# Rope for the first retention head inside the dense stage of a hybrid block kernel, with a place of its own for the returning values

## The chip, the cores and the metric

The kernel runs on one core of one Trainium2 chip. The metric is the device time of one execution in microseconds (us). The time is the median of several executions; a further execution is taken by the hardware profiler, and all rows that are quoted come from such a profiled execution.

A core has five engines that work side by side, each through its own queue of instructions in order: TensorE (PE in the rows, its weight loads PEld), VectorE (DVE), ScalarE (ACT), GpSimd (POOL) and SyncE (SP). They wait for each other by semaphores. SP, ACT and POOL also issue DMA transfers between the main memory and the core's memory (128 partitions). TensorE writes its results into banks of PSUM.

## The reference

One block of a transformer on 512 tokens and 16 leading meta tokens (528 in all, 1024 wide, fp32):

```python
h = concat(meta, x)
h = h + 0.5 * swiglu(rmsnorm(h, ffn1_norm), ffn1_w_gate, ffn1_w_up, ffn1_w_down)
h = h + hybrid_mixer(rmsnorm(h, mix_norm), pos, k_top, w_in, w_ret_out, w_att_out, w_mix_out)
h = h + 0.5 * swiglu(rmsnorm(h, ffn2_norm), ffn2_w_gate, ffn2_w_up, ffn2_w_down)
y = rmsnorm(h, final_norm)[:, 16:]
```

The mixer projects the tokens with one matrix, `w_in`, into: retention queries and keys (`rq`, `rk`, 4 heads of 256), values (`rv`, 4 heads of 512) and gate (`rg`); attention queries, keys and values (`aq`, `ak`, `av`, 8 heads of 128); index queries and key (`iq`, 8 heads of 64; `ik`, one head) with weights `iw`; and two gates `g_ret`, `g_att` of width 1024. Then

```python
yr = retention(rope(rq), rope(rk) / 16, rv)      # scores with a decay by distance, causal, then rmsnorm
yr = (silu(rg) * yr) @ w_ret_out
ya = attention(rope(aq), rope(ak), av, top 128 keys of each query by the index scores, and the meta tokens) @ w_att_out
merged = sigmoid(g_ret) * yr + sigmoid(g_att) * ya
```

Rope multiplies the two halves of each query or key by cosines and sines: `x1 * cos - x2 * sin`, `x2 * cos + x1 * sin`.

## The kernel before

**Arithmetic.** Each fp32 operand is split into a high and a low part. `split` makes the high part by a copy on ACT and the low part by a subtraction on DVE (L117, L118 in the profile; L278, L279 in the pipelined steps). `mm3` (L145) does three matmuls for each product (L153). The activations of the mixer lie split as `xh`, `xl`; weights are loaded on SP into `raw` (L133, two buffers of 1 MB) and split into `whi`, `wlo` (three buffers).

**Order.** The order on TensorE is that of the program everywhere (a manual schedule for PE). In the dense stage ACT and DVE follow the program too; later a scheduler orders ACT, DVE, POOL and SP. `steps_through` (L283) pipelines the dense steps: each step loads its weights four steps ahead (`pre`), has the high parts made two steps ahead (`upper`) and the low parts beside a step (`lower`).

**The dense stage** (in the mixer up to about 572 us). After the first FFN come nine early steps: index queries and keys, the retention queries and keys of head 0. `normed_out` (L868) multiplies these by the norm and writes them to main memory (`fq`, `fs`, `fk`). Then three units of `Values` compute the values of four retention heads and eight attention heads by Strassen's seven products, 14 steps each, and write them to `vst` and `vd` through POOL's queue. After each of the first two units stands a `gate_step` for the retention gate; after the third stand two `rg_step`s (the first two blocks of head 0's `rg`, left in PSUM as `first_rg`) and a `gate_step` for the first block of the attention gate (GA).

**Retention** (pool `rt`, about 572 to 935 us), head by head. For head 0 the queries and keys are loaded back from `fs` and `fk` with the rope tables, and pass `rope_pair` (L1366): four products on DVE (L1371), two sums on POOL (L1374) and two splits. For the others they come from projections `psrq` and `psrk`, which end in the same function. `load_values` (L1320) loads the head's values from `vst` into one of the two `raw` buffers (L1323) and splits them into `vo`. `decayed` (L1413) computes the scores `psst` (L1422) and multiplies them by the decay (L1426) on DVE. Then, for four blocks, `gated` projects `psrg` and `weigh` (L1445) multiplies scores and values (`pspv`, L1442). `ret_out` (L1381) of one head is done during the next head: it projects with `w_ret_out` (`psro`), multiplies by the norm on DVE (L1400) and adds on POOL into `accr` (L1401).

Between these pieces, `step()` takes one piece of background work: in head 0 the index scores (`index_steps`, L1271, matmuls `pssc` L1285, for which `index_ropes`, L1242, ropes the index queries and keys loaded back from `fq` and `fs`), from head 1 on the selection of the top 128 (`select_steps`, L1295, MAX8 and MATCH_REPLACE8 on DVE).

**Attention** (about 935 to 1160 us). Values come from `load_values` again. For each head `scores` (L1599) computes four blocks `psS` (L1612) in the order 3, 2, 1, 0, the block 3 in a two-bank tile and the others in one-bank tiles, and softmaxes them; the next head's `proj_q` and `proj_k` follow, then `transpose_p`, a `wide_gate` (one block of a gate, 24 matmuls, in a two-bank tile) and `weigh_v`.

The output projection, the second FFN and the last norm follow; the change does not touch them.

## Time and profile before

| what | value |
|---|---|
| time, median of 3 runs | 1604.28 us (1603.66 to 1606.98) |
| the profiled execution's own time | 1602.45 us |
| its span, first instruction to last | 1600.7 us |
| mean granted clock of TensorE | 0.979 of full speed |
| PE busy | 1533.6 us (96%) |
| DVE busy | 1088.7 us (68%) |
| ACT busy | 726.6 us (45%) |
| POOL busy | 169.9 us (11%) |
| read and written in main memory | 155.14 MB and 15.75 MB |

How to read the rows further on. The page shows the span in 40 equal slices of 40 us, each with a digit for the busy share in tenths (9 is 90% or more) or the granted clock. A row of the table of stretches has: begin and end, length, then busy time of PE, PEld, DVE, ACT and POOL with the number of instructions in brackets, the granted clock of TensorE, the share of the DMA engines and GB/s. A row of the waits has: the waiting engine and operation, what it waited for, us in total, times, the longest. A row of the chain of waits has: start, length, what the end of the kernel was waiting for at that time. A row of the timeline has: start, length, engine, line, operation, output and input, and in square brackets the idle time of the engine just before it with what ended it. A row of one line's instructions has the shortest, median and longest duration in ns.

### The profile page before, as it was taken

Reading aid. Unit: us, or ns where it says so; the run is one execution under the profiler, and the core shown is the slowest. Engines: PE = TensorE matmul, PEld = TensorE weight load, DVE = VectorE, ACT = ScalarE, POOL = GpSimd, SP = SyncE. Lnnn points to the kernel's source line nnn. Section 1 sums busy time; section 2 is a strip of 40 time slices with the busy share of each in tenths; the row PEclk is TensorE's granted clock in tenths of the full one; section 3 lists DMA queues with packets and bytes.
Section 4 is the critical chain, followed back from the end, with each engine's and each line's share of the span. In section 5 each row is a group of like instructions: output and inputs, shape, how many; then the busy total and the mean of one; then the engine's idle time right before and its main releaser. Section 6 shows DMA issues by size and latency. Waiting matters only on the chain.

```text
span 1600.7 us, 24057 instructions
## 1 busy us (share of the span) xinstructions
PE 1533.6 (96%) x9779; PEld 1380.9 (86%) x9779; DVE 1088.7 (68%) x1652; ACT 726.6 (45%) x1145; POOL 169.9 (11%) x180
## 2 busy tenths in 40 slices
PE   9999999999999948999898989999999999999998
PEld 8999999999888836878687878888888889899996
DVE  4987685876867647795858356655455688577685
ACT  6564362543444424333233336666435445354353
POOL 0000000012101120203223051120001100000000
PEclk9999999999999978999899999999999999999999
DMA  4233223347155251141413143222434223323232
GB/s 160 80 106 106 93 98 101 106 130 259 67 192 184 80 171 49 53 136 38 154 38 110 60 139 90 72 69 80 139 126 137 79 80 105 132 80 132 79 106 92
DMA packets 154302, 172.42 MB, mean 108 GB/s; under 512 B 5008, under 2 KB 130984, under 8 KB 153424
## 3 DMA queue, kind: packets, MB, share of 16 engines
q1 hardware_dynamic: 143824, 147.49, 28.5%
q10 hardware_dynamic: 6880, 12.84, 2.4%
q0 software_dynamic: 3488, 10.58, 1.6%
q8 instruction: 76, 1.25, 0.3%
q14 instruction: 34, 0.28, 0.1%
HBM read 155.14 MB, written 15.75 MB: 107 GB/s over the span
## 4 chain that ended last, share of the span: by engine, by line
PE 85%; DVE 5%; ACT 3%; issue 2%; DMA 2%; POOL 2%; ACTq 0%; POOLq 0%; DVEq 0%
PE psqX L153 13%; PE psd L153 8%; PE psd L1806 7%; PE psqY L153 6%; PE psrg L153 5%; PE psvX L1071 4%; PE psqZ L153 3%; PE psrk L153 3%; PE psu L153 3%; PE psrq L153 3%; PE psmo L153 3%; PE psat L153 3%; PE psgate L153 3%; PE psak L153 3%; PE psaq L153 2%
## 5 line engine op out<-in xcount | busy, mean ns | idle before, releaser
L118 DVE TENSOR_TENSOR wlo<-raw,whi 128x1024 fp32r<-128x1024 f32 (+1 forms) x122 | 143.7, 1178 | 138.8 <-ACT whi L117 137.8
L117 ACT ACTIVATE whi<-raw 128x1024 fp32r<-128x1024 f32 (+1 forms) x122 | 114.4, 939 | 257.5 <-DMA raw<-in_w_in_dram 40.9
L278 ACT ACTIVATE whi<-raw 128x1024 fp32r<-128x1024 f32 (+2 forms) x138 | 121.4, 881 | 110.2 <-PE psd L153 37.5
L279 DVE TENSOR_TENSOR wlo<-raw,whi 128x1024 fp32r<-128x1024 f32 (+2 forms) x138 | 141.0, 1026 | 33.9 <-ACT whi L278 33.9
L153 PE MATMUL psqX<-th,whi 128*128 128x264 f32 (+1 forms) x432 | 122.3, 283 | 0.0
L153 PE MATMUL psqX<-tl,whi 128*128 128x264 f32 (+1 forms) x432 | 122.3, 283 | 0.0
L153 PE MATMUL psqX<-th,wlo 128*128 128x264 f32 (+1 forms) x432 | 122.2, 283 | 0.0
L278 ACT ACTIVATE whi<-wsum 128x1024 fp32r<-128x1024 f32 x72 | 76.3, 1060 | 70.6 <-PE psd L1806 22.0
L279 DVE TENSOR_TENSOR wlo<-wsum,whi 128x1024 fp32r<-128x1024 f32 x72 | 87.7, 1219 | 12.5 <-ACT whi L278 12.5
L153 PEld LDWEIGHTS psqX<-th,whi 128*128 128x128 f32 x432 | 82.1, 190 | 0.3 <-DVE g L492 0.3
L153 PEld LDWEIGHTS psqX<-tl,whi 128*128 128x128 f32 x432 | 82.0, 190 | 0.0
L153 PEld LDWEIGHTS psqX<-th,wlo 128*128 128x128 f32 x432 | 82.0, 190 | 0.0
L153 PE MATMUL psro<-vo,whi 128*128 128x512 f32 x256 | 79.0, 390 | 0.0
L153 PE MATMUL psd<-hl,whi 128*128 128x264 f32 x352 | 71.3, 284 | 0.0
L153 PE MATMUL psd<-hh,wlo 128*128 128x264 f32 x352 | 70.7, 283 | 0.0
L153 PE MATMUL psd<-hh,whi 128*128 128x264 f32 x352 | 70.7, 282 | 0.0
L1806 PE MATMUL psd<-whi,hh 128*128 128x512 f32 x176 | 68.5, 389 | 0.0
L1806 PE MATMUL psd<-wlo,hh 128*128 128x512 f32 x176 | 68.5, 389 | 0.0
L1806 PE MATMUL psd<-whi,hl 128*128 128x512 f32 x176 | 68.5, 389 | 0.0
L252 POOL TENSOR_TENSOR ssum<-ssum,sq 128x528 f32<-128x528 f32 (+1 forms) x14 | 18.4, 1317 | 443.3 <-ACT sq L251 443.3
L153 PEld LDWEIGHTS psro<-vo,whi 128*128 128x128 f32 x256 | 48.0, 188 | 10.0
L153 PE MATMUL psrg<-xh,wlo 128*128 128x512 f32 x128 | 52.6, 411 | 2.5 <-DVE wlo L118 2.5
(434 smaller groups left out, 4654.1 us busy)
## 6 DMA issues: line engine op xcount, KB each, us to landing
raw<-in_ffn_w_up_dram SPq DMA_DIRECT2D x22, 1024.0 KB, 5.0
raw<-in_ffn_w_gate_dram SPq DMA_DIRECT2D x21, 1024.0 KB, 5.0
raw<-in_w_in_dram SPq DMA_DIRECT2D x19, 1024.0 KB, 4.9
raw<-in_w_in_dram SPq DMA_DIRECT2D x31, 512.0 KB, 3.5
raw<-in_ffn_w_down_dram SPq DMA_DIRECT2D x24, 512.0 KB, 4.6
w<-in_w_in_dram SPq DMA_DIRECT2D x24, 512.0 KB, 5.7
raw<-in_ffn_w_down_dram SPq DMA_DIRECT2D x12, 768.0 KB, 4.5
raw<-in_w_ret_out_dram SPq DMA_DIRECT2D x16, 512.0 KB, 3.3
```

What stands on the lines that cost most here:

```text
L117: nc.scalar.activation(hi, src, AF.Copy)
L118: eng.tensor_tensor(lo, src, hi.bitcast(F32), ALU.subtract)
L153: nc.tensor.matmul(o, a[:, k, :], b[:, sl], start=first and k == 0 and i == 0, stop=last and k == nk - 1 and i == 2, skip_group_check=onto)
L252: eng.tensor_tensor(ssum[:, :n], ssum[:, :n], sq[:, :n], ALU.add)
L278: nc.scalar.activation(hi, src, AF.Copy)
L279: return lambda: nc.vector.tensor_tensor(lo, src, hi.bitcast(F32), ALU.subtract)
L1071: nc.tensor.matmul(d[bank_][t], a, b[:, k, :], start=not onto and j + k + m == 0, stop=j + k == 3 and m == 2, skip_group_check=onto)
L1806: nc.tensor.matmul(ps, a[:, bs], m[:, j, :], start=first and i == 0, stop=last and i == 2)
```

## The change

The diff has these parts.

- **Rope of head 0 in the dense stage.** The early activations `hT` become one tile, `hall`, and its pool stays open until retention ends. When `hT` is done with (step 10 of unit 0), `bring` loads the keys and queries of head 0 back into its place, and the rope tables into `ev` tiles. `rope_beside` puts rope operations beside steps 2, 8, 10, 12 and 13 of unit 1 (keys) and unit 2 (queries): six DVE products and sums and two splits each. The roped keys and queries of every head then live in that place (`ret_k`, `ret_q`).
- **The end of the dense stage.** The attention gate's first block is no longer a dense step; it is a `wide_gate` between `proj_q` and the scores of attention head 0. The two `rg_step`s run after the `rt` pool has opened.
- **Values.** `load_values` becomes `fetch_values` (the load) and `split_values`. Head 0 still loads into `raw`; from head 1 on, the load goes into a tile of its own, `vraw` (one buffer), and is issued ahead of the `ret_out` work; the split comes behind `decayed`. In attention the first half is split behind the scores of head 0, the second half is loaded then and split in head 1.
- **Index steps.** In head 0's loop, each block takes one index step behind `psrg` and one behind `weigh`, five in all in place of eight; the rest run in head 1, at its steps and, what is left, ahead of `ret_out`.
- **Attention.** The order of the blocks in `scores` is 2, 1, 0, 3; there are 7 `tmp` buffers in place of 8.

The diff's core:

```diff
+        def bring():
+            hall_r = fp.tile([P, 4352], F32R, tag="hT", name="rqk")
+            for at, c0, width, n in ((ret_k, 0, 576, T), (ret_q, 2304, S, S)):
+                at.extend(tuple(hall_r[:, c0 + (2 * j + i) * width :][:, :n] for j in range(2)) for i in range(2))
+            for i in range(2):
+                nc.sync.dma_start(ret_k[i][0].bitcast(F32), fk[i])
+                nc.sync.dma_start(ret_q[i][0].bitcast(F32), fs[:, 1 + i, :])
+                tables.append(out_tile())
+                nc.sync.dma_start(tables[i], rope[2, i])
+
+        def rope_ops(at, cols):
+            a, b = (p[0].bitcast(F32) for p in at)
+            cs, sn = (t[:, cols] for t in tables)
+            t1, t2 = (room("rope")[:, : cols.stop - cols.start] for _ in range(2))
+            tt = nc.vector.tensor_tensor
+            return [lambda: tt(t1, a, cs, ALU.mult), lambda: tt(t2, b, sn, ALU.mult),
+                    lambda: tt(t1, t1, t2, ALU.subtract), lambda: tt(t2, a, sn, ALU.mult),
+                    lambda: split(t1, *at[0]), lambda: tt(t1, b, cs, ALU.mult),
+                    lambda: tt(t2, t2, t1, ALU.add), lambda: split(t2, *at[1])]
...
-        meanwhile = {0: lambda: (split_xn(range(4, 8), first), normed_out(8)),
+        meanwhile = {10: bring, 0: lambda: (split_xn(range(4, 8), first), normed_out(8)),
...
-        steps += units[1].steps(units[2], {}) + [gate_step(OFF_GR + P, 1)]
-        steps += units[2].steps(None, {}) + [rg_step(0), rg_step(1), gate_step(OFF_GA, KD)]
+        steps += units[1].steps(units[2], rope_beside(ret_k, slice(0, T))) + [gate_step(OFF_GR + P, 1)]
+        steps += units[2].steps(None, rope_beside(ret_q, REAL))
+        n_dense = len(steps)
+        steps += [rg_step(0), rg_step(1)]
...
-    def load_values(i, parts):
-
-        raw = wpool.tile([P, 2048], F32, tag="raw", name="raw", bufs=2).rearrange("p (c t) -> p c t", c=4)
-        nc.sync.dma_start(raw, vst[i].rearrange("p c b d -> p c (b d)"))
+    def split_values(raw, parts):
...
+    def fetch_values(i, raw):
+
+        nc.sync.dma_start(raw, vst[i].rearrange("p c b d -> p (c b d)"))
+        return raw.rearrange("p (c t) -> p c t", c=4)
+
+    def vraw():
+        return vr["pool"].tile([P, 2048], F32, tag="vraw", name="vraw")
...
             if h == 0:
-                qs = [rt.tile([P, S], F32, tag="ossum", name="qs", bufs=2) for _ in range(2)]
-                ks = [tmp() for _ in range(2)]
-                for i in range(2):
-                    nc.sync.dma_start(ks[i], fk[i])
-                    nc.scalar.dma_start(qs[i], fs[:, 1 + i, :])
                 nc.scalar.dma_start(u, decay[h])
-                sgs = [gated(ps) for ps in first_rg]
-                rq = rope_pair(*qs, cos[:, REAL], sin[:, REAL], S, "rq")
-                rk = rope_pair(*ks, cos, sin, T, "rk")
+                place_tails(0)
+                raw = fetch_values(0, wpool.tile([P, 2048], F32, tag="raw", name="raw", bufs=2))
+                for _ in pipe:
+                    pass
+                sgs = [silu_of(ps) for ps in first_rg]
+                rq, rk = ret_q, ret_k
...
                 if h == 1:
                     for _ in bg[0]:
                         pass
                     bg[0] = select_steps()
+                    ixs.close()
+                    ap = accs.enter_context(pool("acc", 1, side="right"))
+                    acc_r.extend(ap.tile([P, S], F32, tag=f"accr{c}", name=f"accr{c}") for c in range(KD))
+                    vr["pool"] = vrs.enter_context(pool("vraw", 1, side="right"))
+                place_tails(h)
+                raw = fetch_values(h, vraw())
                 last_out()
-            place_tails(h)
-            vs = load_values(h, parts)
             o = []
             prob = decayed(rq, rk, u)
+            vs = split_values(raw, parts)
...
                     ps = proj_real(cg, "psrg") if c < 2 else None
+                    if c < 2:
+                        step()
                     if c < 3:
                         weigh(c, vs[c], sgs[c], prob, ssum, o)
                         step()
-                        step()
                     if c < 2:
-                        sgs.append(gated(ps))
+                        sgs.append(silu_of(ps))
...
-            def scores(q, k, order=(3, 2, 1, 0)):
-                for j in order:
+            def scores(q, k):
+                for j in (2, 1, 0, 3):
...
             place_tails(4)
-            vs = load_values(4, [v[:, :4, :] for v in vo])
             k, q = proj_k(), proj_q()
+            wide_gate()
             for h in range(AH):
                 more = h + 1 < AH
                 scores(q, k)
+                if h == 0:
+                    vs = split_values(raw, [v[:, :4, :] for v in vo])
+                    raw = fetch_values(5, vraw())
...
                 pt = transpose_p()
-                if h == 1:
-                    more_vs = load_values(5, [v[:, 4:, :] for v in vo])
                 wide_gate()
                 weigh_v(h, pt, vs[h])
+                if h == 1:
+                    more_vs = split_values(raw, [v[:, 4:, :] for v in vo])
```

More of the change, by code (lines that the diff above doesn't have):

```diff
@@ L528, in mm_tile @@
         return mx["mm"].tile([P, 1024], F32, tag="mm", name=name)
-    with pool("f1") as fp, ExitStack() as later:
+    f1s = ExitStack()
+    fp = f1s.enter_context(pool("f1"))
+    with ExitStack() as later:
         plain_ps = ExitStack()
@@ L556, in gains_in @@
             nc.vector.tensor_copy(gains[:, i : i + n, :].rearrange("p a k -> p (a k)"), pg[:, : n * KD])
-        hT4 = [fp.tile([P, 4, T], F32, tag=f"hT{k}", name=f"hT{k}") for k in range(KD // 4)]
+        hall = fp.tile([P, 4352], F32, tag="hT", name="hT")
+        hT4 = [hall[:, 4 * k * T : 4 * (k + 1) * T].rearrange("p (k t) -> p k t", k=4) for k in range(KD // 4)]
         hT = [hT4[k // 4][:, k % 4, :] for k in range(KD)]
@@ L1177 @@
             sqp.append(sqs.enter_context(pool("sq", 1, side="right")))
-            for _ in pipe:
-                pass
+            for _ in range(n_dense - n_busy):
+                next(pipe)
         dense.close()
@@ L1374, in rope_pair @@
                 nc.gpsimd.tensor_tensor(prod[u], prod[u], prod[v], op)
-                h = rt.tile([P, wide(n)], F32R, tag=f"{name}h{i}", name=f"{name}h")[:, :n]
-                l = rt.tile([P, wide(n)], F32R, tag=f"{name}l{i}", name=f"{name}l")[:, :n]
-                split(prod[u], h, l)
-                outp.append((h, l))
-            return outp
+                split(prod[u], *at[i])
+            return at
         def ret_out(h, o, rn, norm=iter(())):
-            if h == 0:
-                ixs.close()
-                ap = accs.enter_context(pool("acc", 1, side="right"))
-                acc_r.extend(ap.tile([P, S], F32, tag=f"accr{c}", name=f"accr{c}") for c in range(KD))
             cols = Cols(w_ro[h * DV : (h + 1) * DV, :], 0, KD, DV // P)
@@ L1669 @@
                     vs += more_vs
+        vrs.close()
         mgs = ExitStack()
```

48 lines of the change are left out of this document (31 added, 17 removed).

## The prediction, made before the changed kernel had run

> **What bounds the kernel now.** I read the head of the page first, then busy time by stretch, then TensorE's waits, then the chain of waits around the largest hole.
>
> ```profile
> span 1600.7 us, 24057 instructions
> PE   9999999999999948999898989999999999999998
> PEclk9999999999999978999899999999999999999999
> ```
>
> TensorE (PE) is busy nearly everywhere: one hole in the fifteenth slice (560 to 600), small dents up to the twenty-fifth. So a step off TensorE is worth only the TensorE idle time that it ends, plus the lower clock that follows idle time. The stretches with dents (core's span, then PE busy; the number before the DMA share is the granted clock):
>
> ```profile
> 560.00:580.00 20.00, 12.34 (x55) 9.88 (x53) 3.58 (x3) 3.66 (x4) 3.00 (x12) 0.87 0.60 193
> 580.00:600.00 20.00, 4.74 (x17) 3.82 (x18) 16.03 (x17) 7.33 (x10) 7.47 (x5) 0.54 0.44 150
> 600.00:640.00 40.00, 35.31 (x169) 26.36 (x169) 29.46 (x45) 18.47 (x36) 2.55 (x2) 0.87 0.17 52
> 640.00:700.00 60.00, 56.02 (x315) 47.83 (x314) 48.07 (x84) 20.53 (x36) 9.84 (x9) 0.98 0.27 88
> 760.00:820.00 60.00, 53.42 (x244) 44.33 (x243) 45.69 (x85) 18.60 (x28) 11.63 (x9) 0.91 0.34 112
> 820.00:880.00 60.00, 54.05 (x292) 46.94 (x292) 46.51 (x77) 18.09 (x28) 19.73 (x17) 0.94 0.27 87
> 880.00:960.00 80.00, 75.76 (x359) 63.09 (x357) 36.53 (x55) 27.44 (x39) 26.17 (x26) 0.96 0.33 100
> 960.00:1000.00 40.00, 36.11 (x213) 32.72 (x214) 26.49 (x64) 24.19 (x44) 6.46 (x5) 0.96 0.31 90
> ```
>
> ```profile
> PE psst L1422 <- ACT rkh L117: 22.9, 1, 22.9
> PE psst L1422 <- DVE tmp L1426: 7.4, 3, 3.6
> PE psst L1422 <- DVE tmp L1400: 5.3, 2, 3.2
> PE psS L1612 <- ACT aq L117: 4.0, 1, 4.0
> PE psS L1612 <- ACT gate L1354: 3.7, 4, 0.9
> PE psS L1612 <- ACT gate L1561: 2.7, 3, 0.9
> PE psrg L153 <- DVE wlo L118: 2.5, 1, 2.5
> ```
>
> The losses by place are idle time (length minus PE busy) and clock (1 minus the granted clock, where there was work):
> - Head 0's start, 560 to 640: idle 7.66 + 15.26 + 4.69 = 27.6. Clock: 40 x 0.13 = 5.2 in the third row, and about 2 in the second (4.74 of work at 0.54). Some 34.6.
> - Head 1, 640 to 700: idle 4.0, clock 60 x 0.02 = 1.2; 5.2.
> - Head 2, row 760: idle 6.6; clock at most 5.4, some 3.5 of it in work. Head 3, row 820: idle 6.0; clock at most 3.6, some 2 in work. Together 18.1.
> - Attention's start, 880 to 963: idle 4.2 and, of the last row, 3.0 (its other 0.9 is the next item); clock 3.2 + 1.6. 12.0.
> - The seven psS waits for a gate, 3.7 + 2.7 = 6.4.
>
> That is 76 us, all that an edit on this side of TensorE can win. The chain shows what the largest is made of:
>
> ```profile
> 569.40 4.82 DMA raw<-in_w_in_dram
> ...
> 577.15 6.86 DMA qs<-fs
> 584.04 4.67 DVE tmp L1371 x4
> ...
> 594.57 0.65 ACT rkh L117
> 595.22 0.04 issue
> 595.26 4.35 PE psst L1422 x12
> ```
>
> The keys and queries of head 0 are loaded back only once the rt pool opens, behind weights, then pass rope on VectorE (DVE) and GpSimd (POOL) and a split, while TensorE has nothing.
>
> **The change, part by part.** I compared the built orders. TensorE's instructions are as many as before (9564), and its order and waits are the same ahead of the end of the dense stage and again from the last attention heads on. What can differ lies between about 561 and 1150.
>
> *Rope in the dense stage (units 1 and 2).* Added there: 12 DVE rope operations, 4 splits (each one ScalarE (ACT) and one DVE operation), 4 loads back and 2 tables on SP. Their cover is this:
>
> ```profile
> 440.00:520.00 80.00, 80.00 (x464) 66.04 (x463) 56.13 (x53) 37.31 (x42) 7.65 (x12) 1.00 0.54 188
> 520.00:560.00 40.00, 40.00 (x289) 33.27 (x288) 24.48 (x23) 17.24 (x18) 4.28 (x6) 1.00 0.20 77
> L1371 DVE TENSOR_TENSOR tmp<-psrk,cos x6: 693/703/708, 662.7 to 841.4; 128x528 f32<-128x528 f32 x6
> ```
>
> 16 DVE operations by 0.70 are 11 us, and 4 ACT halves by 0.65 are 2.6 us. DVE is busy 80.6 of 120 there, so 39 us are free; weight splits are made two steps ahead, and no point gets more than two operations at once (1.4 us). SP's six extra loads stand between weight loads of a burst that is needed a unit later. I count it as nothing. With the cover gone it costs at most 11 + 2.6 = 13.6; it can't gain.
>
> *Head 0's start.* With keys and queries ready before the dense stage ends, psst has no rope to wait for and follows the last rg step at once: the 22.9 goes. The attention gate that stood there is done later, with the same 24 matmuls, so its work only moves. Next late are the index ropes. In the new order of TensorE, an index group (pssc) stands ahead of the first weigh, so behind psst and one psrg TensorE waits for keys and queries of the index. Their loads stand on SP behind a weight load of 1 MB, and on ACT's queue behind the tails. The last landing then stands before this chain:
>
> ```profile
> 606.78 0.68 DVE L1264 TENSOR_TENSOR tmp<-tmp 64x512 f32<-64x512 f32 x1
> 610.74 0.96 DVE L1252 TENSOR_TENSOR iqa<-iqa,cos 128x768 f32<-128x768 f32 x1 [3.28 <-DMA iqa<-fq]
> 611.61 1.39 DVE L1267 TENSOR_TENSOR ikl<-tmp,ikh 64x512 fp32r<-64x512 f32 x2
> ```
>
> One weight load (4.82), a landing (3.3 to 6.9) and about 5 of DVE (two query multiplications and an add of 0.96, a split of about 0.95, 1.39) make 13 to 17 from psst's end, against some 6 us of psrg: a wait of 7 to 11. The second half of the queries follows behind another weight load; I give it 3 (0 to 8). After such waits the clock falls, here about 5 us. Left are 15 to 24, and outside all bounds 9 to 32; I take 20. The gain is 14.6 (3 to 25).
>
> *Head 1.* psst's products now stand ahead of the values' split on DVE, and psrg's first split is made within the output step, so the 5.2 may go. But three index groups are drained right ahead of psro, whose first bank waits for an ACT relu that now stands behind the split of roped keys: new idle of about 2.5. Net 2.7 (-2 to 5).
>
> *Heads 2 and 3.* The values used to take one of two weight buffers, so psrg's weights came late and DVE stood still:
>
> ```profile
> 771.41 5.96 DMA raw<-in_w_in_dram
> ...
> 778.57 1.23 DVE L118 TENSOR_TENSOR wlo<-raw,whi 128x1024 fp32r<-128x1024 f32 x1 [3.21 <-ACT whi L117]
> ...
> 780.78 2.05 DVE L118 TENSOR_TENSOR vo<-raw,vo 128x1024 fp32r<-128x1024 f32 x1
> ```
>
> With a place of their own the values no longer push that load back, and DVE's 3.2 goes. But psst's product still waits behind weight splits and one vo (2.05) in DVE's queue: DVE is busy 45.69 of 60. The bounds are no gain and all 18.1. I take one 3-us wait in each head, 6 (0 to 12).
>
> *Attention's start.* Before, the values' split (vo, into space that head 3's tmp tiles had held) stands first in ACT's queue until POOL is through:
>
> ```profile
> 946.11 2.01 ACT L117 ACTIVATE vo<-raw 128x1024 fp32r<-128x1024 f32 x2 [5.60 <-POOL pj L1576]
> 948.03 1.04 ACT L117 ACTIVATE whi<-raw 128x1024 fp32r<-128x1024 f32 x1
> ```
>
> The psaq weights stand behind it. In the new order three weight splits come first, so the waits for them go. A gate (24 matmuls, some 5.5 us) now stands between psaq and psS and covers the 4.0 wait for aq, though ACT puts the second half of the values (2.0 us, and its load) ahead of aq's split: 0 to 3 stay. I take 9 of 12 (3 to 12).
>
> *psS order.* Three blocks in other banks come ahead of the one whose bank waits for the gate: 1.3 us of work against 0.9. The wait goes: 6 (0 to 6.4). The transposes now wait for the block that is done last, but 11 us of projections lie between.
>
> **The sum**: 14.6 + 2.7 + 6 + 9 + 6 = 38.3. The profiled execution took 1602.45 (span and 1.75 around it), 1.8 under the median of 1604.28: 1564.1 in its terms, **1566** as a median.
>
> A rule against a row, which the sum doesn't need:
>
> ```profile
> 608.00:612.00 4.00, 1.92 (x12) 1.24 (x11) 1.26 (x2) 2.37 (x5) 0.00 (x0) 1.00 0.36 97
> 612.00:616.00 4.00, 3.33 (x10) 1.70 (x10) 3.94 (x6) 2.04 (x5) 0.00 (x0) 0.52 0.00 0
> ```
>
> Some 2.1 idle in one stretch, and the clock in the next is 0.52. The Trainium skill, page "TensorE: Matmul & The Clock Gate", section "Why this matters for your kernels", says that only idle gaps above about 3 us bring the clock down. By that, the 3-us wait that I leave in head 0 would keep its clock (2 us less) and head 1's 1.2 couldn't be won: 1565. The row contradicts it.
>
> **The rivals.**
> - *The wait only changes its name.* The index loads end so late that head 0 gains 2; in heads 2 and 3 DVE stays the bound (gain 0), head 1 gains nothing; attention's 6 and psS' 6 remain: 14, so 1590. For it: 16.03 of 20 busy on DVE in the row of 580, and the two loads are only moved behind other waits. Against it: the keys and queries (DVE 4.67, the splits) really leave that row.
> - *Slower: a ring of loads in head 0.* Each of the five index groups that stand in the loop waits for a load that SP issues only after the previous weights are split, which waits for TensorE: 4.82 + 6.86 + 2.35 = 14 each, 70, and some 12 of clock. That ends head 0 at 82 in place of 34.6; with the other 23.7 won it is 23.7 slower: 1628. It decides from 58 / 5 = 11.7 per group on. Against it: only two index query loads and the key's follow weights, so the last groups should find theirs in place.
> - *All waits go*: the upper ends, 25 + 5 + 12 + 12 + 6 = 60, so 1544.
> - *The rope isn't hidden*: 13.6 from the forecast, 1580, if units 1 and 2 show idle TensorE.
>
> **How the numbers follow.** Forecast (1550 to 1580) 0.65, with the unhidden rope as its upper end; changed name (1580 to 1600) 0.18; all waits go 0.06; the ring 0.08, about 0.03 at no change. The range, 1550 to 1593, leaves out the last two groups, the best one and the tail of the second, near 0.2. A measurement tells about 0.2% (3 us) from no change. Faster 0.89, same 0.03, slower 0.08.
>
> **What would show it.** Right: no idle ahead of psst; a wait of 7 to 11 at pssc; units 1 and 2 at full PE; no psS row for a gate. Wrong: pssc waits that sum above 20, idle in the dense stage, psst still waiting for DVE by 3 in heads 2 and 3, or a new wait at psro in head 1 above 3.

## The result, and the profile after

| | before | after |
|---|---|---|
| time, median | 1604.66 us (4 runs, 1603.66 to 1606.98) | 1565.12 us (4 runs, 1563.62 to 1567.74) |
| the profiled execution | 1602.45 us | 1567.74 us |
| its span | 1600.7 us | 1566.0 us |
| mean granted clock of TensorE | 0.979 | 0.985 |
| PE busy | 1533.6 us (96%) | 1528.2 us (98%) |

The ratio is 0.9753, with an interval of 0.9736 to 0.9770: the change makes the kernel 2.5% faster. The medians are 39.5 us apart and the profiled executions 34.7. The one of before happened to lie 2.2 under its median, the one of after 2.6 above its own (its granted clock is the lowest of its four, 0.985 against 0.988 to 0.989), so what the traces can account for is 34.7.

The head of the page after, TensorE's row:

```profile
PE   9999999999999979999899999999999999999998
```

The hole in the fifteenth slice has shrunk from a 4 to a 7, and the dents behind it are gone but for one. The busy time by stretch of the kernel after, in the same stretches (length, busy time of PE, PEld, DVE, ACT, POOL, granted clock, DMA share, GB/s):

```profile
440.00:520.00 80.00, 80.00 (x464) 66.04 (x463) 61.00 (x61) 38.39 (x43) 7.53 (x11) 1.00 0.58 201
560.00:580.00 20.00, 17.19 (x87) 13.98 (x85) 8.48 (x15) 9.44 (x15) 1.28 (x2) 1.00 0.74 231
580.00:600.00 20.00, 11.09 (x34) 7.93 (x35) 16.69 (x21) 7.78 (x13) 0.00 (x0) 0.63 0.38 127
600.00:640.00 40.00, 38.17 (x230) 31.75 (x229) 23.20 (x34) 15.34 (x28) 9.22 (x9) 0.97 0.09 29
640.00:700.00 60.00, 57.45 (x281) 48.18 (x280) 54.10 (x100) 22.14 (x36) 4.37 (x3) 0.94 0.38 127
700.00:760.00 60.00, 56.84 (x311) 49.06 (x309) 44.01 (x63) 18.86 (x26) 21.09 (x18) 0.99 0.23 76
760.00:820.00 60.00, 57.87 (x317) 50.76 (x318) 39.02 (x72) 18.67 (x30) 10.26 (x11) 0.95 0.24 79
820.00:880.00 60.00, 56.18 (x264) 47.18 (x263) 44.11 (x76) 21.31 (x32) 14.63 (x12) 0.97 0.31 101
880.00:960.00 80.00, 76.96 (x397) 66.27 (x396) 49.82 (x78) 37.62 (x57) 32.91 (x28) 0.96 0.35 104
```

The first row is the dense stage with the rope in it: TensorE is at 100% and full clock, while DVE rose from 56.13 to 61.00. From 560 to 600 TensorE now works 28.3 of 40 us, where it worked 17.1. TensorE's waits in the kernel after:

```profile
PE pssc L1327 <- ACT ikh L1308: 8.3, 1, 8.3
PE psst L1463 <- DVE tmp L1441: 5.7, 2, 3.2
PE psS L1661 <- ACT aq L117: 3.0, 1, 3.0
PE psst L1463 <- DVE tmp L1467: 2.9, 2, 2.5
PE psrg L153 <- ACT tmp L1330: 2.6, 1, 2.6
PE psro L153 <- ACT tmp L1330: 2.5, 1, 2.5
```

The 22.9 for the roped keys has become 8.3 for the index key, the seven waits for a gate are gone, and two rows are new: `psrg`, 2.6, and `psro`, 2.5, both for a relu of the index scores on ACT (L1330).

Left at each place, worked out as in the prediction (idle time, and 1 minus the granted clock where there was work):

| place | before | forecast | after | how |
|---|---|---|---|---|
| head 0, 560 to 640 | 34.6 | 20 | 18.9 | idle 2.81 + 8.91 + 1.83; clock 11.09 x 0.37 + 40 x 0.03 |
| head 1, 640 to 700 | 5.2 | 2.5 | 6.1 | idle 2.55; clock 60 x 0.06 |
| heads 2 and 3, 700 to 880 | 18.1 | 12 | 13.2 | idle 3.16 + 2.13 + 3.82; clock at most 5.4, less 1.3 that fell on idle time (a row below) |
| attention's start, 880 to 960 (before: to 963) | 12.0 | 3 | 6.2 | idle 3.04; clock 80 x 0.04; none of either from 960 to 1000 |
| psS waits for a gate | 6.4 | 0.4 | 0 | no row |

The gains add up to 15.7 - 0.9 + 4.9 + 5.8 + 6.4 = 31.9 of 34.7. The other 2.8 is not located; the clocks are rounded to 0.01, which is up to 0.3 in a row of 60 us, in both kernels. The clock's share is that of this one execution: the last section shows that the same wait brings more or less of it.

### The profile page after: what moved, and what is told of

It reads as the page before. It is cut to its first block, busy times and chain, and to the rows that moved or that the text cites. A ratio compares the mean times of both kernels' runs of the same rounds, so it can differ in the third digit from the quotient of the medians.

```text
span 1566.0 us, 24024 instructions
## 1 busy us (share of the span) xinstructions
PE 1528.2 (98%) x9779; PEld 1378.4 (88%) x9779; DVE 1092.2 (70%) x1656; ACT 728.1 (46%) x1145; POOL 167.2 (11%) x175
## 4 chain that ended last, share of the span: by engine, by line
PE 86%; DVE 6%; POOL 2%; issue 2%; DMA 1%; ACT 1%; ACTq 0%; POOLq 0%; DVEq 0%
PE psqX L153 13%; PE psd L1859 7%; PE psd L153 7%; PE psqY L153 6%; PE psrg L153 5%; PE psvX L1111 4%; PE psqZ L153 3%; PE psrk L153 3%; PE psu L153 3%; PE psrq L153 3%; PE psga L153 3%; PE psmo L153 3%; PE psat L153 3%; PE psak L153 3%; PE psaq L153 3%; PE psgate L153 2%
## 5 line engine op out<-in xcount | busy, mean ns | idle before, releaser
L118 DVE TENSOR_TENSOR wlo<-raw,whi 128x1024 fp32r<-128x1024 f32 (+1 forms) x123 | 149.7, 1217 | 121.7 <-ACT whi L117 120.6
L153 PE MATMUL psrg<-xh,whi 128*128 128x512 f32 x128 | 53.5, 418 | 3.7 <-ACT tmp L1330 2.6
```

The costliest lines, as they stand in the source:

```text
L118: eng.tensor_tensor(lo, src, hi.bitcast(F32), ALU.subtract)
L153: nc.tensor.matmul(o, a[:, k, :], b[:, sl], start=first and k == 0 and i == 0, stop=last and k == nk - 1 and i == 2, skip_group_check=onto)
```

## The theory and its rivals

The theory is the prediction's sum: five places, each with a cause of its own, and nothing lost in the dense stage. Rivals are that the rope in the dense stage costs something there after all; that the new order alone, not the earlier rope, ended the large wait; and, at each place where a wait stayed, another engine as its cause. Each expectation below names the readings that it sets against each other. All kernels compute the whole reference; x_rope2 does some products twice. Each run of a group was timed against the kernel before on the same chip (medians 1604.81 to 1605.94), so ratios are compared.

## The experiments

### Rope of head 0 back at its old time (x_roplate)

The loads and the place of the keys and queries stay as in the kernel after; only the rope operations go back behind the dense stage.

```diff
-        steps += units[1].steps(units[2], rope_beside(ret_k, slice(0, T))) + [gate_step(OFF_GR + P, 1)]
-        steps += units[2].steps(None, rope_beside(ret_q, REAL))
+        steps += units[1].steps(units[2], {}) + [gate_step(OFF_GR + P, 1)]
+        steps += units[2].steps(None, {})
...
-                rq, rk = ret_q, ret_k
+                rq = rope_pair(*(p[0].bitcast(F32) for p in ret_q), cos[:, REAL], sin[:, REAL], S, ret_q)
+                rk = rope_pair(*(p[0].bitcast(F32) for p in ret_k), cos, sin, T, ret_k)
```

> The changed kernel, but the rope and split of head 0's keys and queries are done at the start of retention; they are still loaded back inside the values' stage. Theory A (most of the old 22.9 us wait was the loads; what the rope costs at that place is largely taken back from the wait for the index keys, which stands next): psst waits 6 to 8 us, the wait at pssc falls from 8.3 to 2 to 4, in all 1 to 9 us slower than the changed kernel, about 1569. Theory B (the rope itself was the price): 15 us slower, about 1580. Theory C (only the loads counted): no difference.

Measured: 1573.82 us, ratio 0.9798 (0.9783 to 0.9813), some 7 us more than the kernel after by the ratios. TensorE's waits:

```profile
PE psst L1463 <- ACT rqk L117: 7.9, 1, 7.9
PE pssc L1327 <- ACT ikh L1308: 4.6, 1, 4.6
```

The wait for roped keys is back, though the data lay in the core's memory early. It is 7.9 and not 22.9, and the index wait behind it shrinks from 8.3 to 4.6 (2 to 4 was expected), since it is partly covered. So of the 15.7 won at head 0, about 7 are lost again without the early rope; the rest comes with the earlier loads and the new order, which were not tried apart.

### The rope's products done twice in the dense stage (x_rope2)

Eight more DVE operations in units 1 and 2, the same result.

```diff
+            def twice(*a):
+                tt(*a)
+                tt(*a)
-            return [lambda: tt(t1, a, cs, ALU.mult), lambda: tt(t2, b, sn, ALU.mult),
+            return [lambda: twice(t1, a, cs, ALU.mult), lambda: twice(t2, b, sn, ALU.mult),
...
```

> The changed kernel, with each of the rope's eight products in the dense stage done twice: 8 more operations of 0.70 us on DVE, 5.6 us. Theory A (hidden: DVE is 70 to 76 per cent busy there and TensorE full): TensorE stays at 100 per cent from 440 to 560 us, time unchanged within 2 us. Theory B (the cover is nearly used up): some 3 to 6 us slower, with idle TensorE in that stage.

Measured: 1564.86 us, ratio 0.9738 (0.9724 to 0.9753), not to be told from the kernel after. The same stretch of the dense stage:

```profile
440.00:520.00 80.00, 80.00 (x465) 66.02 (x464) 63.65 (x66) 38.58 (x43) 7.53 (x11) 1.00 0.59 201
```

DVE is busy 2.7 us longer there (63.65 against 61.00), and 3.5 longer from 520 to 560 (31.24 against 27.77); TensorE is busy for all of both stretches, as before. The rope is hidden there, and so would half as much again be. The equal time alone would not show it, for behind the dense stage the waits changed: in place of the 8.3 at `pssc`, `psrg` waits 5.6 for a high part of its weights and 4.2 for a low one.

### Index ropes ahead of the rg steps (x_idx)

Before looking at the edit, this is how the 8.3 arises. First ACT's timeline of the kernel after (start, length, engine, line, operation; ACTq marks a DMA issue), then the chain of waits in that stretch, then TensorE's timeline:

```profile
568.03 0.35 ACTq L1292 DMA_DIRECT2D iqb<-fq  x1
...
575.37 0.31 ACTq L1292 DMA_DIRECT2D iqb<-fq  x1
585.58 1.28 ACT L1308 ACTIVATE ikh<-tmp 64x512 fp32r<-64x512 f32 x2 [2.36 <-DMA iqb<-fq]
```

```profile
575.37 4.33 DMA iqb<-fq
```

```profile
586.26 1.44 PE L1327 MATMUL pssc<-ikh,iqh 64*128 64x512 f32 x2 [8.29 <-ACT ikh L1308]
```

The small loads of the first index queries are issued by ACT, in order with its own work. The first goes at 568.03, the last only at 575.37, because splits of values and scores stand between, and for 2.35 of these ACT itself stands still until DVE has multiplied the scores (L1467). It lands at 579.70. DVE then ropes queries and key, with a weight split in between, and only at 585.58 can `ikh` be split: the row names the DMA, but what ended just ahead of it is the key's last sum on DVE, at 585.55. TensorE has stood still for 8.29 when `pssc` begins. The edit puts the whole of `index_ropes` one place further up:

```diff
                 raw = fetch_values(0, wpool.tile([P, 2048], F32, tag="raw", name="raw", bufs=2))
+                index_ropes()
                 for _ in pipe:
...
             if h == 0:
-                index_ropes()
                 bg[0] = index_steps()
```

> The changed kernel, but the loads and rope of the index queries and keys stand ahead of the last rg steps in the program, so that ACT's and SP's queues issue them earlier. Theory A (the 8.3 us at pssc are these loads, issued late in ACT's queue between its splits): the wait falls to 0 to 3, and the clock behind it: 5 to 12 us faster. Theory B (another input of the first block, the values' split or the weights, is late by as much): 0 to 3 us faster.

Measured: 1560.32 us, ratio 0.9723 (0.9709 to 0.9738), some 5 us less than the kernel after; the intervals touch (0.9736 to 0.9738). The 8.3 is gone; new, and smaller, are TensorE's waits of 2.6 for the index weights (`wt`) and of 1.9 in front of a `psst`. ACT's timeline of this kernel:

```profile
567.05 2.19 ACTq L1292 DMA_DIRECT2D iqb<-fq  x4
```

The four loads now go one behind the other in 2.19 us. What is left at head 0, worked out as in the table, falls from 18.9 to 14.0, which is the 5. So the wait was a matter of the place in ACT's queue, as the prediction had it in its words "on ACT's queue behind the tails", though it is splits that stood ahead. The other part, SP's loads behind a weight load, is moved by the same edit and was not tried alone; the chain of the kernel after names ACT's load.

### The old order of psS (x_order)

```diff
-                for j in (2, 1, 0, 3):
+                for j in (3, 2, 1, 0):
```

> The changed kernel with the score blocks in the old order 3, 2, 1, 0. Theory A (the order alone took the seven waits for the gate away): seven waits of about 0.9 us at psS come back, 6 us slower, about 1571. Theory B (other parts of the change took them away): no difference.

Measured: 1572.36 us, ratio 0.9791 (0.9775 to 0.9807), some 6 us more than the kernel after. TensorE's waits:

```profile
PE psS L1661 <- ACT gate L1610: 3.6, 4, 0.9
PE psS L1661 <- ACT gate L1394: 2.7, 3, 0.9
```

The seven waits come back one by one, 6.3 in all, against 6.4 before the change. This term of the sum stands alone.

### The attention gate behind the scores of attention head 0 (x_nogate)

```diff
-            wide_gate()
             for h in range(AH):
...
                 scores(q, k)
+                if h == 0:
+                    wide_gate()
```

> The changed kernel with the new gate of attention head 0 behind the scores in place of ahead of them. Theory A (the gate's 5.5 us cover the way to aq): the wait at the first psS grows from 3.0 to about 8.5 us, 5 to 8 us slower. Theory B (the way to aq stands in ACT's queue behind the gate's weights, and without the gate it is shorter by as much): the wait stays about 3 and the time unchanged.

Measured: 1571.75 us, ratio 0.9785 (0.9771 to 0.9800), some 5 us more than the kernel after. TensorE's wait:

```profile
PE psS L1661 <- ACT aq L117: 8.4, 1, 8.4
```

The wait for `aq` grows by 5.4, just the work of the gate that stood there (the prediction put it at 5.5). The gate covers; what it does not cover is the 3.0 that stayed.

### What makes aq late: GpSimd (x_akdve) or the second half of the values (x_f5)

In the kernel after, first POOL's timeline at the start of attention, then ACT's:

```profile
914.24 8.99 POOL L1442 TENSOR_TENSOR accr<-accr,tmp 128x512 f32<-128x512 f32 x4
...
926.15 1.34 POOL L1243 TENSOR_TENSOR tmp<-tmp,sin 128x528 f32<-128x528 f32 x1
```

```profile
928.27 0.64 ACT L117 ACTIVATE ak<-tmp 128x528 fp32r<-128x528 f32 x1 [4.57 <-DVE tmp L1244]
...
929.89 0.59 ACT L1240 ACTIVATE tmp<-psaq 64x512 f32<-64x512 f32 x1
...
930.99 1.99 ACT L117 ACTIVATE vo<-vraw 128x1024 fp32r<-128x1024 f32 x2
933.20 0.63 ACT L117 ACTIVATE aq<-tmp 128x512 fp32r<-128x512 f32 x1 [0.21 <-DVE tmp L1244]
```

The first key's sine product stands in POOL's queue behind the last sums of retention and the issues of the tails. ACT stands still 4.57 in front of `ak`'s split, and the first step of `aq`'s rope (L1240) stands behind that split. The values' split `vo` does stand ahead of `aq`, but it is over at 932.98, and `aq` then still waits 0.21 for its own rope. Two edits, the first with that one product on DVE, the second with the load of the second half of the values later in the program:

```diff
-    def rope_swap(ps, cos, sin, half, n):
+    def rope_swap(ps, cos, sin, half, n, eng=nc.gpsimd):
...
-        nc.gpsimd.tensor_tensor(b[:, :n], b[:, :n], sin, ALU.mult)
+        eng.tensor_tensor(b[:, :n], b[:, :n], sin, ALU.mult)
...
-            k, q = proj_k(), proj_q()
+            k, q = proj_k(nc.vector), proj_q()
```

> The changed kernel, but the sine product of the first attention key is done on DVE in place of POOL. Theory A (the 3.0 us at the first psS come from POOL, which adds into accr until 923 us and issues the tails' loads until 926, and holds ak and, behind it in ACT's queue, aq): the wait falls to 0 to 1.5, with the clock behind it 1 to 5 us faster. Theory B (the second half of the values ahead of aq's split on ACT and DVE is what holds it, as the prediction had it): unchanged.

```diff
                     vs = split_values(raw, [v[:, :4, :] for v in vo])
-                    raw = fetch_values(5, vraw())
...
                 pt = transpose_p()
+                if h == 0:
+                    raw = fetch_values(5, vraw())
```

> The changed kernel, but the second half of attention's values is loaded a head's scores later, so that its split no longer stands ahead of aq's on ACT and DVE. Theory A (POOL's queue holds the way to aq, since the product moved to DVE took the wait from 3.0 to 1.3): the wait at the first psS falls by no more than the one DVE operation, 3.0 to 1.5 to 2. Theory B (the prediction's: the values' half is the cause): it falls to 0 to 1.

Measured: x_akdve 1563.64 us, ratio 0.9745 (0.9725 to 0.9764), within the interval of the kernel after; x_f5 1564.93 us in its one run. So only the traces can tell. x_f5 doesn't test what it was made for. SP issues the load in it as early as in the kernel after (there at 922.12), and the split of that half (928.82 to 930.81) still stands ahead of `aq`'s (931.04) on ACT:

```profile
922.16 0.34 SPq L1401 DMA_DIRECT2D vraw<-vst  x1
```

The edit moved the load in the program and not in the order that ran. TensorE's wait for `aq` in x_akdve, and in x_drain (below), which leaves this place as it is in the kernel after:

```profile
PE psS L1661 <- ACT aq L117: 1.3, 1, 1.3
```

```profile
PE psS L1665 <- ACT aq L117: 2.0, 1, 2.0
```

The wait of 3.0 isn't fixed. POOL's four sums take 8.99 in the kernel after, but 7.99 in x_akdve and x_f5 and 8.11 in x_drain, and the wait follows them: in the ten kernels that have the product on POOL and the gate in its place, sums of 8.99 to 9.06 go with waits of 2.9 to 3.1 (five kernels), 7.99 to 8.11 with 1.9 to 2.1 (four, x_f5 among them), and 7.06 with 1.5 (x_skip). At equal sums the wait is 2.0 without an edit and 1.3 with the product on DVE. In x_drain and x_akdve a second wait of 0.4, for the low part of `aq`, comes behind the first, so that in all 3.0 becomes 2.4 and, with the product moved, 1.7. So POOL carries a part of the wait, 0.6 by the length of its sums and 0.7 by the product behind them. What holds the other 1.7 was not tried; ahead of the product on DVE stands the split of the first half of the values, 4.54 for two.

### Where the values live, and where they are split (x_raw, x_vfirst)

x_raw lets the values of heads 1 to 3 take one of the two weight buffers again; x_vfirst splits them ahead of `decayed` again, but keeps their own place.

```diff
-                raw = fetch_values(h, vraw())
                 last_out()
+                raw = fetch_values(h, wpool.tile([P, 2048], F32, tag="raw", name="raw", bufs=2))
```

> The changed kernel, but the values of heads 1 to 3 come again through one of the two weight buffers, loaded behind the output step's loads; their split stays behind the scores. Theory A (a place of their own keeps psrg's weights early): DVE stands still again for 2 to 3 us before psrg's weight split, psst and psrg wait longer, 3 to 12 us slower. Theory B (the order of the splits brought the gain): no difference within 2 us.

```diff
             o = []
+            if h:
+                vs = split_values(raw, parts)
             prob = decayed(rq, rk, u)
-            vs = split_values(raw, parts)
+            if not h:
+                vs = split_values(raw, parts)
```

> The changed kernel, but in heads 1 to 3 the values are split ahead of the scores, so that both halves (1.2 to 2.05 us each) stand before psst's product on DVE. Theory A (DVE's queue ends last there): the psst waits of 2.5 and 3.2 us grow by 1 to 2 each, and head 1 gets one: 2 to 9 us slower. Theory B (the load's place alone counts): no difference within 2 us.

Measured: x_raw 1570.82 us, ratio 0.9788 (0.9766 to 0.9809); x_vfirst 1568.79 us, ratio 0.9778 (0.9761 to 0.9795). Both are slower than the kernel after by their ratios, some 6 and 4 us, but both intervals overlap its own a little. TensorE's waits in x_raw, then in x_vfirst:

```profile
PE psrg L153 <- DVE wlo L118: 4.3, 1, 4.3
PE psst L1463 <- DVE tmp L1441: 4.2, 2, 2.2
```

```profile
PE psst L1463 <- DVE tmp L1467: 8.1, 4, 3.7
```

The 4.3 of x_raw stands in head 1 alone (at 676). In heads 2 and 3, of which the prediction said that their own place for the values would free the weights, all waits at `psst` are 4.2, against 8.2 in the kernel after (5.7 and one of 2.5): there the place wins nothing, and why the waits are longer with it was not tried. Over the whole kernel TensorE's idle time is no longer in x_raw (37.0 against 37.8); it is busy longer (1533.2 against 1528.2), so what x_raw loses isn't idle time. The order matters in heads 2 and 3, as x_vfirst shows: the scores' products behind the values' splits cost 8.1 against 2.9 in all, 6.2 against 2.5 in these two heads, and head 1 gets one of 1.5.

### DVE in heads 2 and 3 (x_skip)

What holds `psst` in heads 2 and 3 of the kernel after, on DVE and then on TensorE:

```profile
747.37 0.67 DVE L1441 TENSOR_TENSOR tmp<-psro,rn 128x512 f32<-128x512 f32 x1
...
750.42 0.67 DVE L1441 TENSOR_TENSOR tmp<-psro,rn 128x512 f32<-128x512 f32 x1
...
754.01 0.67 DVE L1441 TENSOR_TENSOR tmp<-psro,rn 128x512 f32<-128x512 f32 x1
...
755.07 2.06 DVE L118 TENSOR_TENSOR wlo<-raw,whi 128x1024 fp32r<-128x1024 f32 x1
...
757.58 0.68 DVE L1441 TENSOR_TENSOR tmp<-psro,rn 128x512 f32<-128x512 f32 x1
```

```profile
752.21 0.39 PE L153 MATMUL psro<-vo,wlo 128*128 128x512 f32 x1
752.44 3.36 PE L1463 MATMUL psst<-rqk 128*128 128x512 f32 x18
758.31 1.05 PE L1463 MATMUL psst<-rqk 128*128 128x256 f32 x6 [2.51 <-DVE tmp L1441]
```

For each of the eight columns of `ret_out` DVE has a product, a selection step of two operations and a split. In head 2 the products follow each other by 3.05 five times (as 747.37 to 750.42, with a split of 128x512 between) and then by 3.59 and 3.57 (a split of 128x1024, the weights of `psrg`). TensorE needs twelve matmuls by about 0.23 (752.21 to 752.44), 2.8. DVE falls behind, most in the last two, and the fourth `psst` waits for the bank that the last product frees (757.58 + 0.68 = 758.26). In head 3 five columns take 2.92, the sixth 3.44, and the last 4.57, for there half of the values' split (1.22, at 844.55) stands ahead of the last product. The edit takes the selection step away behind the last two columns (it is done at a later `step()`; `h` is the head whose output is projected, so 1 and 2 stand for heads 2 and 3):

```diff
-                step(ins)
+                if h not in (1, 2) or c < KD - 2:
+                    step(ins)
```

> The changed kernel, but the selection takes no step behind the last two columns of the output step in heads 2 and 3 (the steps are taken later), so that DVE is freed of about 1.1 us for each. Theory A (in heads 2 and 3 psst waits for its place in DVE's queue): the waits of 5.7 and 2.9 us at psst fall together by 2 to 4, with the clock behind them 2 to 6 us faster. Theory B (what ends last is the weights' load or POOL): unchanged within 2 us.

Measured: 1567.30 us, ratio 0.9768 (0.9753 to 0.9782): no gain. TensorE's wait, and the last selection step on DVE ahead of the last product in head 2:

```profile
PE psst L1464 <- DVE tmp L1441: 6.0, 2, 3.5
```

```profile
754.84 0.55 DVE L1344 MAX8 top<-score 128x8 f32<-128x384 f32 x1
```

My expectation of a gain failed, and the trace shows why: the edit took no work off the way to the bank. Between the last products (754.24 and 757.82, 3.58 apart as before) a step still stands; in head 3, too, seven steps stand ahead of the last product in both kernels. What is gone is the step that followed the last product in the kernel after (at 758.18). So the waits for the products of `psst` (L1467 before, L1468 here) fell from 2.9 to 1.1, while those of `psrg` for the same products rose from 1.1 to 2.2, and the bank's stayed. The run says nothing for or against the lag; the last experiment tries it.

### The index groups ahead of ret_out in head 1 (x_drain)

The new `psro` wait: relus of the drained index groups stand in ACT's queue behind the split of the roped keys. Two more steps are taken earlier in head 1:

```diff
                 last_weigh()
                 step()
+                if h == 1:
+                    step()
                 qb = proj_real(cols, "psrq")
                 step()
+                if h == 1:
+                    step()
```

> The changed kernel, but the two index groups that head 1 takes right ahead of its output step are taken earlier, behind the first weigh and the second query projection. Theory A (psro's bank waits for the relu of these groups, which stands behind the split of the roped keys in ACT's queue): the 2.5 us at psro go, with the 3 of clock behind it 3 to 6 us faster. Theory B (the earlier places wait as long for a bank): unchanged.

Measured: 1563.74 us, ratio 0.9743 (0.9727 to 0.9759), some 1.5 us less than the kernel after, within the intervals. Head 1's stretch:

```profile
640.00:700.00 60.00, 59.85 (x312) 51.05 (x313) 55.25 (x101) 22.91 (x37) 4.59 (x3) 1.00 0.44 138
```

The wait and the low clock behind it are gone from this stretch (57.45 at 0.94 in the kernel after). That is worth 6 here, and the time shows only 1.5. From 560 to 700 the idle time fell by 1.9, from 16.1 to 14.2, for part of it moved (`pssc` waits of 1.1, a `psrg` wait of 2.9 for 2.6). And the low clock was not a fixed price: in other kernels the same `psro` wait cost less of it, or none (last section).

### All together (x_all)

x_idx, x_akdve and x_drain, and in heads 2 and 3 a selection step only behind every other column of `ret_out`, with a second step at each gate in its place:

```diff
-                step(ins)
+                if h not in (1, 2) or c % 2 == 0:
+                    step(ins)
...
                 sg = silu_of(proj_real(cg, "psrg"))
                 step()
+                if h in (2, 3):
+                    step()
```

> The changed kernel with four edits together: the index loads earlier, the first attention key's product on DVE, head 1's index groups earlier, and in heads 2 and 3 the selection takes a step behind every other column of the output step only, with a second step behind each gate of these heads in its place. The first three measured alone 5, 1 and 2 us. Theory A (in heads 2 and 3 DVE falls behind by 0.8 us in each of eight columns, so that leaving out every other step there lets it keep up): both waits of about 2.5 and that of 3.2 us at psst fall below 1, worth 5 to 10 us with the clock; in all 12 to 18 us faster than the changed kernel, 1547 to 1553. Theory B (the waits there don't hang on the selection): 6 to 9 us faster in all, 1556 to 1559, with psst waiting as before.

Measured: 1547.77 us (5 runs, 1543.66 to 1549.20), ratio 0.9632 (0.9618 to 0.9645). It beats both kernels, the one after by some 19 us by the ratios. Head 2's stretch, and two rows of DVE's timeline, a column without the step and the product behind it:

```profile
700.00:760.00 60.00, 60.00 (x332) 52.56 (x331) 47.35 (x78) 21.24 (x32) 22.79 (x17) 1.00 0.36 118
```

```profile
739.22 1.21 DVE L118 TENSOR_TENSOR wlo<-raw,whi 128x1024 fp32r<-128x1024 f32 x1
741.00 0.69 DVE L1441 TENSOR_TENSOR tmp<-psro,rn 128x512 f32<-128x512 f32 x1 [0.57 <-PE psro L153]
```

In the second row DVE waits for TensorE (0.57): it is no longer the slower of the two, and head 2's `psst` waits are gone, which all stand in x_idx, x_akdve and x_drain (5.7 for the bank in each). Four selection steps stand ahead of the last product there, in place of seven. So DVE's lag over the columns was the cause, which x_skip had left open; in the kernel after it grows in head 2 by about 0.25 in each of five columns and by 0.8 in two, not by 0.8 in each, as I expected. A column without its step saves the split's delay too: it takes 1.21 here and 2.06 above, since POOL's add begins behind it (at 739.38). The three edits that were run alone won about 8 together; the other 11 or so are put down to the fourth, which was not run alone. Head 3 keeps a wait of 2.2 (`psrg`), and in head 0, as in x_idx, `psst` has a new one of 2.3. At attention's start 2.3 stay, by another cause: the values' split now waits 1.37 for its load, ahead of `aq` in ACT's queue (it begins at 912.52, and `aq`'s behind it at 914.43).

## Why the prediction was right, and where its terms were off

The forecast was 1566, the median is 1565.12. That closeness is partly luck: in the terms of the profiled executions the sum of 38.3 was 3.6 too large against 34.7, and the scatter of the two executions gave it back. Two of its five terms were mis-sized, head 1 and attention's start, both by the clock behind a wait that stayed.

- **Dense stage, 0.** Right, and x_rope2 shows room for more.
- **Head 0, left 20.** Measured 18.9. "A wait of 7 to 11" was 8.3, the second, given 3, was 2.6, and "about 5" of clock was 5.3. The cause of the first is shown by x_idx. The second stands at `psrg`, whose bank waits for a relu; ahead of that on ACT stands the split of the second half of the queries, whose load SP issued behind a weight load (at 584.97, landed 5.46 later), as the prediction had it. The ring of loads didn't arise: there is one `pssc` wait.
- **Head 1, net 2.7.** The step "new idle of about 2.5" was right to the hundredth (2.53, `psro`). What failed is that only idle was written down: in the profiled execution the low clock behind the new wait costs 3.6 more, so 6.1 stay where 2.5 were forecast. The prediction had added clock behind head 0's waits and not here. How much of it falls due is partly luck: behind the same wait x_rope2 has none.
- **Heads 2 and 3, 6 of 18.1.** "One 3-us wait in each head" stayed, and more: 2.5 twice in head 2 and 3.2 in head 3. 4.9 was won. The size held, half of the reason did not: x_raw shows that the values' own place wins nothing there. The gain hangs on the order (x_vfirst). Of what stayed, only one 2.5 waits for `psst`'s products, as the prediction said; the 5.7 wait for the bank of the last product of `ret_out`, that is, for DVE's 3.05 to 3.57 for a column and, in head 3, for a half of the values' split. The prediction's own sign of being wrong, `psst` waiting for DVE by 3 in these heads, was met in head 3; it contradicts the 3-us waits that the sum left there.
- **Attention's start, 9 of 12.** 5.8 was won. "0 to 3 stay" was met at its end, 3.0, but "I take 9" left no clock behind it, which took 3.2 (1.6 in x_roplate and x_rope2, behind a wait of 3.0 as well). The cause named, the values ahead of `aq` on ACT, was wrong: they are split in time (932.98 against 933.20), and `aq` waits for its own rope. POOL's queue carries some 1.3 of the wait (x_akdve and the length of the sums); 1.7 stays open. Only in x_all, with POOL's product gone, do the values hold `aq` up.
- **psS order, 6.** Measured 6.4, and 6 to undo (x_order).

The rule that the prediction weighed (the Trainium skill, page "TensorE: Matmul & The Clock Gate", section "Why this matters for your kernels": no drop below idle gaps of about 3 us) would have kept the clock behind head 1's 2.53. The row of that place, below, shows 0.50, as the prediction's row had it. But the row of x_rope2 shows 1.00 behind the same wait, as the rule has it. So neither reading holds in every kernel here.

## What to carry to other kernels

When a wait at TensorE stays or is newly made, price it with the half clock that can follow it, and as a range: behind the same wait of 2.5 us the kernels here lost 0, 1.7 or 3.4 us more. A load whose issue stands in an engine's own queue is as late as the work ahead of it there, so put issues ahead of splits; x_idx won some 5 us by such a move (of issues on ACT and SP together). Where two engines go column by column, compare their time for a column (DVE 3.05 to 3.57, TensorE 2.8). And see from the trace that an edit changed what it was meant to: x_skip took away a step that stood behind the product waited for, and x_f5 moved nothing, so neither tested its theory.

## What the runs showed of the hardware

**A short wait can bring half clock.** Busy time by stretch, of the kernel after around the `psro` wait of 2.53 (644.9 to 647.5) and around `psst` waits of 2.5 in head 2:

```profile
640.00:647.00 7.00, 4.92 (x42) 4.05 (x40) 5.22 (x7) 2.98 (x6) 3.02 (x2) 0.96 0.13 29
647.00:653.00 6.00, 5.53 (x13) 4.37 (x14) 3.33 (x8) 1.67 (x6) 0.00 (x0) 0.50 0.35 147
653.00:660.00 7.00, 7.00 (x31) 5.76 (x31) 6.43 (x13) 1.46 (x3) 0.00 (x0) 0.98 0.24 78
759.00:766.00 7.00, 4.24 (x18) 3.16 (x17) 6.97 (x13) 2.12 (x6) 0.62 (x1) 0.51 0.43 144
```

and of x_vfirst, behind a wait of 1.5 (in the three us before, the clock is 0.90):

```profile
674.00:677.00 3.00, 3.00 (x9) 2.33 (x8) 2.93 (x9) 0.73 (x3) 0.00 (x0) 0.53 0.82 302
```

If the clock is either full or half, the time at half is twice the length by what is missing: 0.56 + 6.0 + 0.28 = 6.84 in the first three rows together, 6.86 in the fourth, and 0.60 + 2.82 = 3.42 in x_vfirst. They are one or two times 3.42 or so. In the fourth row 2.76 of the 7 are idle, so some 2.1 of the 3.43 lost fall on work and 1.3 don't, which the table above uses. The Trainium skill, page "TensorE: Matmul & The Clock Gate", section "What's actually happening", gives a free-running window of 3413 ns; these lengths agree with it. But the same wait isn't always followed by them. The `psro` wait is 2.52 to 2.54 in eleven kernels. Behind it, the clock that is missing from 2 us ahead of its end to 8 behind adds up to 3.4 us in five of them (the kernel after, x_idx, x_nogate, x_raw, x_skip), to 1.7 in three (x_order, x_akdve, x_f5) and to none in three (x_roplate, x_rope2, x_vfirst), as in x_rope2, where the wait ends at 647.47:

```profile
647.50:651.50 4.00, 4.00 (x18) 3.31 (x19) 3.58 (x8) 1.38 (x4) 0.00 (x0) 1.00 0.39 162
```

These are the halves of two, one and no lengths of 3.42. So the length of the wait doesn't decide it, and what does stays open: x_akdve's wait of 1.3 was not followed by half clock (its granted clock is 1.00 from 926 to 940), x_vfirst's 1.5 was.

**DVE and GpSimd hold each other up.** The split of 128x1024 takes 1.21 in x_all's row and 2.06 in that of the kernel after at 755.07, where one of POOL's adds runs from 754.76 for 1.29. The Trainium skill, page "SBUF — State Buffer", section "SBUF: two separate sides", says that a DVE instruction with two inputs from that memory and a GpSimd one that reads it lock each other out for the whole instruction. By that the split would begin at 756.05 and end at 757.26; the trace has 757.13. So the adds of `ret_out`, which TensorE never waits for, lengthen the split in each of DVE's columns in head 2 by 0.85 (the smaller one, 128x512, takes 1.53, and 0.68 at 725.89, where POOL is idle). POOL pays too: its four sums at attention's start took 7.06 to 9.06, where one alone took 1.28 to 1.30 in head 2.
